# Joining the chain's products with one moving operand in a chunked RWKV-7 recurrence on one core

## The chip, the cores and the metric

The kernel runs on one core of one Trainium2 chip. The metric is the device time of one execution in microseconds (us). TensorE (PE in the profile) multiplies a stationary operand, the weights, by a moving operand; a weight load (PEld) goes ahead of each product. VectorE is DVE, ScalarE is ACT, GpSimd is POOL. Each engine works through its own instructions in the order in which they stand in its program and waits where an operand is not ready.

## The reference, cut to what matters

The reference is a whole layer: projections, a bidirectional RWKV-7 recurrence, an RG-LRU branch, output projections and a mixture of experts. The change lies in the recurrence alone:

```python
def step(s, inp):
    r_t, w_t, k_t, v_t, kk_t, a_t = inp
    s_kk = jnp.einsum('bhvk,bhk->bhv', s, kk_t)
    s = (s * w_t[:, :, None, :] - s_kk[..., None] * (kk_t * a_t)[:, :, None, :]
         + v_t[..., None] * k_t[:, :, None, :])
    return s, jnp.einsum('bhvk,bhk->bhv', s, r_t)
```

There are 16 heads of 64, a forward and a backward pass, 256 context tokens and 1024 latent tokens. Only the latent tokens give an output.

## The kernel before, in words

The recurrence is `phase_b`. It runs in chunks of 64 tokens. A group `n` is 128 tokens (two chunks) of 4 heads in both directions (`e` = 0, 1); there are 40 groups, ten for each of four sets of heads (`pr, g = divmod(n, 10)`), and `g` = 0, 1 are context tokens without an output, `g` > 1 latent tokens with one. For each group and direction `stage_e` makes the scaled keys (`bk`), `stage_i` the scaled queries (`qr`: columns 0 to 63 the key side, 64 to 127 the receptance with which the output is read), the masked products `st1` and `st2`, and the inverse `gf` of the chunk's triangular system, by many small bf16 products (lines 880 and 896). That work doesn't depend on the state.

The state goes through `chain(n)`, which calls `step(n, i)` for the two chunks: 80 steps in all, 64 of them with an output (`out`). One half of the partitions (`h` = 0, 1) of `rv` holds the state and the other half the values v, the other way round for the other `h`; so a product over all 128 partitions of `rv` adds a term of the state and one of v. A step, for each `h` and its four `units` (direction and head):

- line 995: `st1` times `rv` (128 rows by 64 weight columns), the right side of the system; DVE (line 996) and ACT (line 997) copy it to `z`
- line 1011: the receptance half of `qr` times the state in `rv` (64 by 64), the state's part of the output, only in steps with an output
- line 1017: `gf` times `z` (64 by 64), the solve, into the same PSUM columns from which `z` was copied; lines 1018 and 1019 write the result into `rv` in place of the state
- line 1026: one half of `st2` times `rv`, the state's update, to which DVE (line 1028) adds the decayed state `sp` that POOL made (line 1005)
- line 1035: the other half of `st2` times the same `rv`, added to line 1011's result; ACT (line 1039) or DVE (line 1041) takes the output to `y`

PSUM holds one bank (2 KB for each partition) for each `h`, `p2[h]`, of two halves. `start` opens an accumulation: it makes the next products of that bank and those partitions overwrite what stands there, and later ones add.

The order of the work is written out by a small planner: generators yield times, `PERIOD` units to a group, and the instructions get their priorities from these. A group's `stage_i` starts 55 units (`LEAD_I`) ahead of its chain, so three groups ahead, and `qr`, `st1`, `st2` and `pc` have four buffers (`NST`). PE's own order mixes the chain's products with the bf16 products of later groups.

Of the kernel before, what the change touches and what calls it, by code (L numbers as in the profile page):

```python
# [9 lines left out]
F32 = mybir.dt.float32  # L10
# [3 lines left out]
AF = mybir.ActivationFunctionType  # L14
OP = mybir.AluOpType
# [3 lines left out]
P = 128  # L19
# [635 lines left out]
def phase_b(S):  # L655

    nc, tc, A, scr, col, mk = S.nc, S.tc, S.A, S.scr, S.col, S.mk
# [7 lines left out]
    C = 64  # L665
    H = ((slice(0, 64), slice(64, 128)), (slice(64, 128), slice(0, 64)))
    QC = (slice(0, 64), slice(64, 128))
    V, G_, A_ = nc.vector, nc.gpsimd, nc.scalar
# [21 lines left out]
    for e in range(2):  # L690
        m = pk.tile([P, 4, 65], F32, name=f"m65{e}")
# [3 lines left out]
        t = pk.tile([P, 2, 4, 65], F32, name=f"cb{e}")  # L695
# [4 lines left out]
    for i in range(6):  # L700
        t = pk.tile([P, 4, P], BF16, name=f"hmx{i}")
        G_.memset(t, 0.0)
        XH.append(t)
    for i in range(NB):
        X = Prog()
        for nm in ("mid", "lo", "u"):
            t = pk.tile([P, 4, P], BF16, name=f"{nm}x{i}")
# [109 lines left out]
    def stage_i(n, e):  # L817

        pr, g = divmod(n, 10)
        alloc_i(n)  # L820
        G, k = GRP[n], 2 * n + e
        X, xh = XB[k % NB], XH[k % 6]
# [7 lines left out]
        kw = dict(skip_group_check=True)  # L830

        r = new("r", dt=F32, bufs=1)
        hm, mid, lo = new("hm"), new("mid", bufs=3), new("lo", bufs=3)
        for h in range(2):
            sr, tr = H[h]
            pg = front([P, 4, P], "pg")
            for j in range(4):
                cols = slice(0, 128) if g > 1 else slice(0, 64)
                nc.tensor.matmul(pg[:, j, cols], G.bk[sr, e, j, 64 * h:64 * h + 128], G.qr[sr, e, j, cols],  # L839
                                 start=True, stop=True)  # L840
            w = G.st1[:, h, e]
            V.tensor_mul(w, pg[:, :, 0:64], bc(mk("strict", e)))
            A_.activation(hm[sr], w[sr], AF.Copy)  # L843
            G_.tensor_tensor(r[sr], w[sr], hm[sr], op=OP.subtract)  # L844
            A_.activation(w[sr], G.qr[sr, e, :, 0:64], AF.Copy)
            if g > 1:
                V.tensor_mul(G.st2[:, h, e, :, QC[1 - h]], pg[:, :, 64:128], bc(mk("incl", e)))
            yield 1.4
# [16 lines left out]
        for h in range(2):  # L865
            sr, b0 = H[h][0], 64 * h
# [42 lines left out]
        u = u8  # L909
        for it in range(7):  # L910
# [5 lines left out]
            u = pi.tile([P, 4, C], BF16, name="u", tag=f"u{k % NB}")  # L916
# [67 lines left out]
    def step(n, i):  # L984

        pr, g = divmod(n, 10)
        G, T = GRP[n], TILE[pr]
        last, out = g == 9 and i == 1, g > 1
        units = [(e, a, 2 * a + (i if e == 0 else 1 - i)) for e in range(2) for a in range(2)]
        kw = dict(skip_group_check=True)  # L990
        p2 = [psC.tile([P, 2, 2, 2, C], F32, name=f"p2{h}", tag=f"p2{h}") for h in range(2)]
        z = pf.tile([P, 2, 2, C], F32, name="z", tag="z", bufs=1)
        for h in range(2):
            for e, a, j in units:
                nc.tensor.matmul(p2[h][H[h][0], 1, e, a], G.st1[:, h, e, j], G.rv[:, h, e, a, i], start=True, stop=True)
        V.tensor_copy(z[0:64], p2[0][0:64, 1])
        A_.activation(z[64:128], p2[1][64:128, 1], AF.Copy)
        if not last:
            sp = pf.tile([P, 2, 2, C], F32, name="sp", tag="sp", bufs=1)
            for h in range(2):  # L1000
                sr = H[h][0]
                pcs = G.pc[sr].rearrange("p e (a c) -> p e a c", a=2)
                for e in range(2):
                    k = i if e == 0 else 1 - i
                    G_.tensor_tensor(sp[sr, e], G.rv[sr, h, e, :, i],  # L1005
                                     pcs[:, e, :, k:k + 1].to_broadcast([64, 2, C]), op=OP.mult)
        for h in range(2):
            if out:
                sr, tr = H[h]
                for u, (e, a, j) in enumerate(units):  # L1010
                    nc.tensor.matmul(p2[h][tr, 0, e, a], G.qr[sr, e, j, 64:128], G.rv[sr, h, e, a, i],
                                     start=(u == 0), stop=False, **kw)
        yield 3
        for h in range(2):
            sr = H[h][0]
            for e, a, j in units:
                nc.tensor.matmul(p2[h][sr, 1, e, a], G.gf[sr, e, j], z[sr, e, a], start=True, stop=True, **kw)
        V.tensor_copy(G.rv[0:64, 0, :, :, i], p2[0][0:64, 1])
        A_.activation(G.rv[64:128, 1, :, :, i], p2[1][64:128, 1], AF.Copy)
        yield 3  # L1020
        rv, i1 = (G.rv, 1) if i == 0 else (None if last else GRP[n + 1].rv, 0)
        for h in range(2):
            sr = H[h][0]
            if not last:
                for u, (e, a, j) in enumerate(units):
                    nc.tensor.matmul(p2[h][sr, 0, e, a], G.st2[:, h, e, j, QC[h]], G.rv[:, h, e, a, i],
                                     start=(u == 0), stop=(u == 3), **kw)
                V.tensor_tensor(rv[sr, h, :, :, i1], p2[h][sr, 0], sp[sr], op=OP.add)  # L1028
        if out:
            s = 2 * (g - 2) + i  # L1030
            lo_, hi_ = min(s, 15 - s), max(s, 15 - s)
            for h in range(2):
                r = H[h][1]
                for u, (e, a, j) in enumerate(units):
                    nc.tensor.matmul(p2[h][r, 0, e, a], G.st2[:, h, e, j, QC[1 - h]], G.rv[:, h, e, a, i],
                                     start=False, stop=(u == 3), **kw)
                y = T.y[r, :, lo_:hi_ + 1:hi_ - lo_].rearrange("p a e v -> p e a v")
                if s < 8:
                    A_.activation(y, p2[h][r, 0], AF.Copy)
                else:  # L1040
                    V.tensor_tensor(y[:, ::-1], p2[h][r, 0], y[:, ::-1], op=OP.add)
        yield 4

    def finish(n):
# [74 lines left out]
    def alloc_i(n):  # L1119
        G = GRP[n]  # L1120
        if hasattr(G, "st1"):
            return
        pr, g = divmod(n, 10)
        G.pc = pf.tile([P, 2, 4], F32, name=f"pc{n}", tag="pc", bufs=NST)
        G.qr = pf.tile([P, 2, 4, P], F32, name=f"qr{n}", tag="qr", bufs=NST)
        G.st1 = pf.tile([P, 2, 2, 4, C], F32, name=f"st1_{n}", tag="st1", bufs=NST)
        G.st2 = pf.tile([P, 2, 2, 4, P], F32, name=f"st2_{n}", tag="st2", bufs=NST)


# [17 lines left out]
    with ExitStack() as s0:  # L1147
        gp = s0.enter_context(tpool(tc, name="gp", bufs=1))
        load_y(S, "yb", [7], lambda k: gp, S.y)
        for j in range(KT):  # L1150
            n = 59 + j
# [6 lines left out]
            z = product(nc, S.psz.tile([P, 2, 512], F32, name="zb", tag="zl"), S.W.pop(n), S.y)  # L1158
# [4 lines left out]
    pf = pool("pf", 1, side="right")  # L1163
    pi = pool2("pi", 2, side="right")
    psC = pool("psC", 1, space=PSUM)
    psI = pool2("psI", 1, space=PSUM, side="right")
    gnx = pf.tile([64, 32], F32, name="gnx")
    nc.sync.dma_start(gnx, A["gnx"])
    S.early = False
    left = [2 * NG]  # L1170

# [5 lines left out]
    for n in range(NG):  # L1177
        t = n * PERIOD
# [6 lines left out]
    while events:  # L1185
        t, k, gen = heapq.heappop(events)
# [22 lines left out]
NST = 4  # L1209
# [715 lines left out]
```

## Time and profile before

| | |
|---|---|
| median of three runs | 3358.96 us (3342.54 to 3366.52) |
| the profiled execution | 3349.37 us, of which the span is 3347.6 us |
| PE busy | 3021.7 us, 90% of the span |
| DVE busy | 2175.8 us, 65% |
| ACT busy | 1516.2 us, 45% |
| POOL busy | 1237.7 us, 37% |
| mean granted TensorE clock | 0.921 of full speed |

A busy time is an average over stages. The recurrence lies between about 1012 us and 2343 us of the span. The granted clock has two levels, 2.4 GHz (1.0) and 1.2 GHz (0.5); a clock between them in a row is a mean over a stretch that has both. In the trace an fp32 product is two records of PE, two passes over its columns, each with a weight load of its own; a transpose (line 868) and a bf16 product are one. The records' ends are modelled and overlap, so what one record costs is read from the distance of starts, not from its length.

### The profile page before, as it was taken

The numbers are of one execution on the slowest core, as the hardware profiler recorded it, in microseconds if no ns is written. First come the engines' busy times: TensorE is split into PE (matmuls) and PEld (weight loads), VectorE is DVE, ScalarE is ACT, GpSimd is POOL, SyncE is SP. The second block draws the span as 40 slices with busy tenths as digits, with TensorE's granted clock in tenths as the row PEclk, the third lists the DMA queues.
The fourth block names the chain that finished last, engine by engine and source line by source line (L and its number), as shares of the span: only waits on it lengthen the run. The fifth ranks groups of instructions, "written<-read, shape, count | busy, mean of one in ns | idle before, by whom it ended". The sixth has DMA issues, their size and how long they took to land. (4 is left out here: it accounts for less than half of the span.)

```text
span 3347.6 us, 67005 instructions
## 1 busy us (share of the span) xinstructions
PE 3021.7 (90%) x26407; PEld 2288.2 (68%) x26407; DVE 2175.8 (65%) x4155; ACT 1516.2 (45%) x3127; POOL 1237.7 (37%) x1517
## 2 busy tenths in 40 slices
PE   7999998899998999999999999999879599999981
PEld 4877776777777888778878887888767343444430
DVE  6768998977537788888877788877559311111115
ACT  4465556565615666566666665765321000000003
POOL 1022333334416555565455555653113212111114
PEclk9999999999996899899987997989989799999995
DMA  5423336432352111222122112312532788688885
GB/s 213 139 97 120 123 121 202 145 110 77 126 181 83 49 50 48 80 77 60 44 81 71 49 50 76 89 32 80 186 135 100 315 349 341 263 359 320 327 345 218
DMA packets 265464, 496.61 MB, mean 148 GB/s; under 512 B 34690, under 2 KB 188002, under 8 KB 239484
## 3 DMA queue, kind: packets, MB, share of 16 engines
q1 hardware_dynamic: 243804, 443.16, 37.5%
q0 software_dynamic: 21280, 48.28, 3.9%
q8 instruction: 251, 4.11, 0.5%
q14 instruction: 129, 1.06, 0.1%
HBM read 437.37 MB, written 83.83 MB: 156 GB/s over the span
## 5 line engine op out<-in xcount | busy, mean ns | idle before, releaser
L1628 PE MATMUL ph<-r,xT 128*64 128x256 f32 (+1 forms) x2176 | 366.1, 488 | 36.9 <-DVE yo L1652 10.4
L234 PE MATMUL zl<-h_hi,wlo 128*128 128x512 f32 x944 | 328.3, 402 | 17.3 <-DVE wlo L157 17.3
L230 PE MATMUL zl<-h_hi,whi 128*128 128x512 f32 x944 | 327.6, 402 | 3.3 <-ACT acc L408 2.7
L232 PE MATMUL zl<-h_lo,whi 128*128 128x512 f32 x944 | 328.4, 402 | 0.6 <-DVE rstd L287 0.5
L1628 PEld LDWEIGHTS ph<-r,xT 128*64 128x64 f32 x2176 | 165.9, 138 | 231.6 <-issue 186.9
L1653 POOL DMA_INDIRECT scr_yx<-yo,sidx x50 | 50.8, 1016 | 500.8 <-DVE yo L1652 342.8
L839 PE MATMUL pg<-qr,bk 64*128 64x128 f32 (+1 forms) x1280 | 216.8, 315 | 15.8 <-DVE bk L800 6.6
L234 PEld LDWEIGHTS zl<-h_hi,wlo 128*128 128x128 f32 x944 | 180.9, 192 | 55.3 <-DVE wlo L157 19.8
L1617 ACT ACTIVATE xT<-pxt 128x512 f32<-128x512 f32 x37 | 22.1, 597 | 426.1 <-DVE hT L1640 337.6
L230 PEld LDWEIGHTS zl<-h_hi,whi 128*128 128x128 f32 x944 | 180.3, 192 | 43.0 <-issue 3.7
L232 PEld LDWEIGHTS zl<-h_lo,whi 128*128 128x128 f32 x944 | 181.5, 192 | 38.2 <-issue 1.4
L844 POOL TENSOR_TENSOR r<-st,hm 64x256 f32<-64x256 f32 x160 | 115.8, 724 | 240.9 <-ACT hm L843 237.4
L839 PEld LDWEIGHTS pg<-qr,bk 64*128 64x128 f32 x1280 | 182.1, 215 | 30.9 <-issue 6.6
L411 DVE SCALAR_TENSOR_TENSOR acc<-zt,drv,acc 128x960 f32<-128x960 f32 (+3 forms) x142 | 170.7, 1208 | 9.1 <-ACT acc L408 5.4
L1005 POOL TENSOR_TENSOR sp<-rv,pc 64x128 f32<-64x128 f32 x304 | 133.9, 458 | 89.2 <-DVE rv L1028 72.4
L896 PE MATMUL pu<-u,n 128*128 128x64 bf16 x2240 | 157.9, 201 | 3.8 <-DVE n L906 2.2
L157 DVE TENSOR_TENSOR wlo<-wraw,whi 128x1024 fp32r<-128x1024 f32 x67 | 101.1, 1509 | 85.0 <-ACT whi L156 81.2
L896 PEld LDWEIGHTS <-n 128*128 128x128 bf16 x2240 | 125.8, 103 | 36.1 <-issue 15.7
L1640 DVE COPY hT<-pht 128x256 f32<-128x256 f32 x32 | 13.6, 424 | 202.3 <-PE pht L1639 202.2
L918 ACT ACTIVATE u<-pu 128x256 bf16<-128x256 f32 x280 | 104.8, 380 | 84.4 <-PE pu L896 81.1
L920 DVE TENSOR_TENSOR u<-pu,u 128x256 bf16<-128x256 f32 x280 | 114.3, 416 | 25.0 <-PE pu L896 21.5
L783 POOL TENSOR_SCALAR km<-cb,ka 128x128 f32<-128x128 f32 x160 | 96.7, 612 | 75.6 <-ACT cb L777 73.9
(457 smaller groups left out, 8280.5 us busy)
## 6 DMA issues: line engine op xcount, KB each, us to landing
r<-in_e_w_dram SPq DMA_DIRECT2D x192, 1024.0 KB
wraw<-in_w_in_dram SPq DMA_DIRECT2D x59, 512.0 KB
adr<-in_w_ada_dram SPq DMA_DIRECT2D x32, 512.0 KB
zk<-scr_zk SPq DMA_DIRECT2D x80, 128.0 KB
kk<-scr_kk SPq DMA_DIRECT2D x80, 128.0 KB
lp<-scr_lp SPq DMA_DIRECT2D x80, 128.0 KB
v<-scr_zv SPq DMA_DIRECT2D x80, 128.0 KB
wada<-in_w_ada_dram SPq DMA_DIRECT2D x8, 1024.0 KB
```

What stands on the lines that cost most here:

```text
L157: nc.vector.tensor_sub(lo, raw, hi.bitcast(F32))
L230: nc.tensor.matmul(pz, z.hi[:, k], h_hi[:, k, t0:t0 + n], start=(k == 0), stop=False)
L232: nc.tensor.matmul(pz, z.hi[:, k], h_lo[:, k, t0:t0 + n], start=False, stop=False)
L234: nc.tensor.matmul(pz, z.lo[:, k], h_hi[:, k, t0:t0 + n], start=False, stop=(k == KT - 1))
L411: nc.vector.scalar_tensor_tensor(o, i, mures[:n, r, j:j + 1], o, op0=OP.mult, op1=OP.add)
L839: nc.tensor.matmul(pg[:, j, cols], G.bk[sr, e, j, 64 * h:64 * h + 128], G.qr[sr, e, j, cols], start=True, stop=True)
L844: G_.tensor_tensor(r[sr], w[sr], hm[sr], op=OP.subtract)
L896: nc.tensor.matmul(pt[:, j], l[:, j], r_ if len(r_.shape) == 2 else r_[:, j], start=first, stop=True, **kw)
L918: A_.activation(u, pt, AF.Copy)
L920: V.tensor_tensor(u, pt, u8, op=OP.add)
L1005: G_.tensor_tensor(sp[sr, e], G.rv[sr, h, e, :, i], pcs[:, e, :, k:k + 1].to_broadcast([64, 2, C]), op=OP.mult)
L1628: nc.tensor.matmul(ph[HALF[h]].rearrange("p a b c -> p (a b c)")[:, c], x[:, k], w13(e, k)[:, h, c], start=(k == 0), stop=(k == KT - 1))
```

## The change

The diff joins products that have the same moving operand: lines 995 and 1011 both multiply by `rv` before the solve, lines 1026 and 1035 by `rv` after it. `st1` grows from 64 to 128 columns: 64 hold the system's right side as before, the other 64 the receptance half of `qr` on the state's partitions and zeros on the others. One product with 128 weight columns fills both halves of the partitions of the bank. `st2` had both halves already. So that the output's accumulation can go on in one half of the bank, the solve is written to the other half; its `start` makes the update that follows overwrite on the state's partitions.

`st1` is no longer taken from a pool: four tiles `ST1` are set to zero once by POOL, ahead of the stage. ACT's copy out of `qr` (line 845) takes 128 columns in place of 64 where there is an output. `qr` is now read by `stage_i` alone and has one buffer in place of four.

```diff
-            w = G.st1[:, h, e]
+            w = G.st1[:, h, e, :, QC[h]]
             V.tensor_mul(w, pg[:, :, 0:64], bc(mk("strict", e)))
             A_.activation(hm[sr], w[sr], AF.Copy)
             G_.tensor_tensor(r[sr], w[sr], hm[sr], op=OP.subtract)
-            A_.activation(w[sr], G.qr[sr, e, :, 0:64], AF.Copy)
+            if g > 1:
+                w = G.st1[sr, h, e].rearrange("p j (b c) -> p j b c", b=2)
+                A_.activation(w[:, :, ::-1] if h else w, G.qr[sr, e].rearrange("p j (b c) -> p j b c", b=2), AF.Copy)
+            else:
+                A_.activation(w[sr], G.qr[sr, e, :, 0:64], AF.Copy)
...
+        both = slice(0, P)
         for h in range(2):
-            for e, a, j in units:
-                nc.tensor.matmul(p2[h][H[h][0], 1, e, a], G.st1[:, h, e, j], G.rv[:, h, e, a, i], start=True, stop=True)
+            m, c = (both, both) if out else (H[h][0], QC[h])
+            for u, (e, a, j) in enumerate(units):
+                nc.tensor.matmul(p2[h][m, 1, e, a], G.st1[:, h, e, j, c], G.rv[:, h, e, a, i], start=(u == 0), stop=True, **kw)
...
-        for h in range(2):
-            if out:
-                sr, tr = H[h]
-                for u, (e, a, j) in enumerate(units):
-                    nc.tensor.matmul(p2[h][tr, 0, e, a], G.qr[sr, e, j, 64:128], G.rv[sr, h, e, a, i],
-                                     start=(u == 0), stop=False, **kw)
...
-            for e, a, j in units:
-                nc.tensor.matmul(p2[h][sr, 1, e, a], G.gf[sr, e, j], z[sr, e, a], start=True, stop=True, **kw)
-        V.tensor_copy(G.rv[0:64, 0, :, :, i], p2[0][0:64, 1])
-        A_.activation(G.rv[64:128, 1, :, :, i], p2[1][64:128, 1], AF.Copy)
+            for u, (e, a, j) in enumerate(units):
+                nc.tensor.matmul(p2[h][sr, 0, e, a], G.gf[sr, e, j], z[sr, e, a], start=(u == 0), stop=True, **kw)
+        V.tensor_copy(G.rv[0:64, 0, :, :, i], p2[0][0:64, 0])
+        A_.activation(G.rv[64:128, 1, :, :, i], p2[1][64:128, 0], AF.Copy)
...
         for h in range(2):
-            sr = H[h][0]
+            m, c = (both, both) if out else (H[h][0], QC[h])
+            for u, (e, a, j) in enumerate(units):
+                nc.tensor.matmul(p2[h][m, 1, e, a], G.st2[:, h, e, j, c], G.rv[:, h, e, a, i], start=False, stop=True, **kw)
             if not last:
-                for u, (e, a, j) in enumerate(units):
-                    nc.tensor.matmul(p2[h][sr, 0, e, a], G.st2[:, h, e, j, QC[h]], G.rv[:, h, e, a, i],
-                                     start=(u == 0), stop=(u == 3), **kw)
-                V.tensor_tensor(rv[sr, h, :, :, i1], p2[h][sr, 0], sp[sr], op=OP.add)
+                sr = H[h][0]
+                V.tensor_tensor(rv[sr, h, :, :, i1], p2[h][sr, 1], sp[sr], op=OP.add)
...
-                for u, (e, a, j) in enumerate(units):
-                    nc.tensor.matmul(p2[h][r, 0, e, a], G.st2[:, h, e, j, QC[1 - h]], G.rv[:, h, e, a, i],
-                                     start=False, stop=(u == 3), **kw)
...
-        G.qr = pf.tile([P, 2, 4, P], F32, name=f"qr{n}", tag="qr", bufs=NST)
-        G.st1 = pf.tile([P, 2, 2, 4, C], F32, name=f"st1_{n}", tag="st1", bufs=NST)
+        G.qr = pi.tile([P, 2, 4, P], F32, name=f"qr{n}", tag="qr", bufs=1)
+        G.st1 = ST1[n % NST]
...
+    ST1 = [pf.tile([P, 2, 2, 4, P], F32, name=f"st1_{i}") for i in range(NST)]
+    for t in ST1:
+        G_.memset(t, 0.0)
```

The reads of the output (lines 1039 and 1041) take the other half of the bank and are otherwise the same.

The order on PE, at a step's first products and its solve in the middle of the stage. Before (in a row's name, `p_...` is the bank of one `h`, `64x64` the size of the product's result; the bf16 rows of line 896 belong to later groups' inverses):

```order
L896 MATMUL pu<-u,n_19538 128x64
L995 MATMUL p_21175<-rv_20062,st_19_18722 64x64 x4
L1011 MATMUL p_21176<-rv_20062,qr_18721 64x64 x4
L1017 MATMUL p_21176<-z,gf_19880 64x64 x4
L896 LDWEIGHTS n_19538
```

After, the first products of a step (lines 918, 872, 884 and 900 are lines 914, 868, 880 and 896 of before, lines 1001 and 1025 the joined products):

```order
L884 MATMUL ph<-x_18131,n_17913 128x8
L1001 MATMUL p_18756<-rv_17773,st_0_7303 128x64 x4
L872 MATMUL pt<-ident,bk_18540 128x64 x4
L1001 MATMUL p_18757<-rv_17773,st_0_7303 128x64 x4
L918 LDWEIGHTS idb
L918 MATMUL pu<-u_17696,idb 128x256
```

The solve of the same step, some 35 rows further on:

```order
L884 LDWEIGHTS n_17913
L884 MATMUL ph<-x_18182,n_17913 128x8
L1017 MATMUL p_18756<-z,gf_17600 64x64 x4
L1017 MATMUL p_18757<-z,gf_17600 64x64 x4
L900 LDWEIGHTS n_17305
L900 MATMUL pu<-u,n_17305 128x64
```

Line 1011's product no longer stands between the first products and the solve; the first products' results are 128 by 64 and lie among products of the same 128 by 128 weights, and the solve alone keeps 64 by 64.

The order on POOL at the stage's start (`km`, `bk` and `pc` are the keys and decays of the first groups, `rv` the state that is set to zero). Before:

```order
L798 TENSOR_TENSOR bk_6658<-km,ip 128x4x64
L814 COPY pc_7303<-pp 128x4
L1106 MEMSET rv_8008 64x2x64 x3
L862 TENSOR_TENSOR bk_7367<-bk_6658,pc_7303 128x4x128
L1106 MEMSET rv_8008 64x2x64
L1005 TENSOR_TENSOR sp<-rv_8008,pc_7303 64x128 x2
```

After (line 1103 is line 1106 of before):

```order
L798 TENSOR_TENSOR bk_6658<-km,ip 128x4x64
L1169 MEMSET st_0_7303 128x2048
L1169 MEMSET st_1_7304 128x2048
L1169 MEMSET st_2_7305 128x2048
L1169 MEMSET st_3_7306 128x2048
L814 COPY pc_7311<-pp 128x4
L1103 MEMSET rv_8014 64x2x64 x4
```

The four new settings to zero stand between the first group's keys and its `pc`, `rv` and `sp`.

## Rows read from the trace of the kernel before

**Rows 1.** Windows over the recurrence: us, then busy (instructions) by engine, clock, DMA.
```profile
1041.00:2343.00 1302.00, 1229.91 (x17430) 1068.50 (x17429) 1062.42 (x2721) 823.96 (x2217) 716.79 (x1102) 0.89 0.22 62
1000.00:1200.00 200.00, 182.85 (x2156) 158.43 (x2154) 146.14 (x369) 115.64 (x311) 113.72 (x180) 0.78 0.21 62
1200.00:1400.00 200.00, 187.07 (x2837) 162.75 (x2836) 170.94 (x437) 130.76 (x354) 115.53 (x175) 0.95 0.23 66
1600.00:1800.00 200.00, 187.43 (x2523) 161.28 (x2523) 164.12 (x410) 125.78 (x330) 117.15 (x177) 0.86 0.25 72
```

**Rows 2.** Waits, 1041 to 2343 us: waiter <- releaser, us in total, times, longest.
```profile
PE pu L914 <- DVE u L920: 9.4, 12, 2.0
...
DVE st L842 <- PE pg L839: 53.7, 57, 3.0
```

**Rows 3.** Groups by line and form, 1000 to 2345 us: count, busy us, mean ns, idle before.
```profile
L995 PE MATMUL p<-rv,st 128*64 128x64 f32 x1280 | 118.5, 242 | 2.2 <-DVE y L1041 1.8
L1026 PE MATMUL p<-rv,st 128*64 128x64 f32 x1216 | 106.3, 246 | 1.8 <-DVE rv L1018 1.2 <-ACT rv L1019 0.2
L1017 PE MATMUL p<-z,gf 64*64 64x64 f32 x1280 | 105.5, 237 | 0.0
L1011 PE MATMUL p<-rv,qr 64*64 64x64 f32 x1024 | 87.6, 232 | 0.5 <-DVE z L996 0.5
L1035 PE MATMUL p<-rv,st 128*64 128x64 f32 x1008 | 86.6, 242 | 1.8 <-DVE rv L1028 1.4
L845 ACT ACTIVATE st<-qr 64x256 f32<-64x256 f32 x160 | 65.9, 412 | 24.2 <-POOL r L844 21.6
L777 ACT ACTIVATE cb<-pl 128x512 f32<-128x512 f32 x79 | 47.0, 595 | 46.9 <-PE pl L775 41.1 <-DVE ip L799 4.9 <-DVE hmx L855 0.3
L811 DVE TENSOR_TENSOR qr<-pp,kk 128x256 f32<-128x256 f32 x80 | 43.2, 541 | 8.4 <-ACT pp L795 4.1 <-PE p L1011 3.4
L1106 POOL MEMSET rv<- 64x128 f32 x16 | 2.8, 198 | 63.6 <-PE zb L1242 59.6 <-PE p L1035 3.7
```

**Rows 4.** PE in order of time: start, us, line, tiles, weights, moving, records.
```profile
1503.32 0.56 PE L995 MATMUL p<-rv,st 128*64 128x64 f32 x6
1503.82 0.40 PE L896 MATMUL pv<-t,hmx 128*128 128x128 bf16 x4
1504.14 0.33 PE L995 MATMUL p<-rv,st 128*64 128x64 f32 x2
...
1504.51 0.57 PE L1017 MATMUL p<-z,gf 64*64 64x64 f32 x7
```

**Rows 5.** The same view in a later stage, the router's products.
```profile
2516.63 0.73 PE L1490 MATMUL plg<-rw,xT 128*128 128x36 f32 x5
2517.18 0.28 PE L1480 MATMUL px<-vv,po 128*128 128x64 bf16 x4
2517.30 0.39 PE L1490 MATMUL plg<-rw,xT 128*128 128x36 f32 x2
2517.53 0.48 PE L1506 MATMUL z<-wo_hi,m_hi 128*128 128x512 f32 x1
```

**Rows 6.** One record's length by line: least, median, most ns.
```profile
L1017 PE MATMUL p<-z,gf x1280: 218/218/366, 1089.8 to 2343.7; 64*64 64x64 f32 x183
L1490 PE MATMUL plg<-rw,xT x128: 194/279/407, 2501.2 to 2612.3; 128*128 128x36 f32 x128
```

**Rows 7.** POOL's setting to zero of 1024 columns, whole span.
```profile
L383 POOL MEMSET ada<- 128x1024 f32 x4 | 3.8, 957 | 0.3 <-issue 0.3
```

**Rows 8.** Windows: a stretch at the full clock and the one behind it at half.
```profile
1549.00:1658.30 109.30, 105.30 (x1636) 91.72 (x1635) 93.42 (x240) 71.55 (x195) 59.37 (x98) 1.00 0.18 53
1658.30:1685.60 27.30, 27.30 (x264) 23.36 (x264) 15.93 (x44) 12.68 (x32) 11.47 (x14) 0.50 0.19 54
```

**Rows 9.** Windows: the last 5 us before two falls of the clock.
```profile
1393.90:1398.90 5.00, 3.46 (x60) 2.88 (x57) 4.91 (x13) 4.53 (x13) 1.47 (x2) 1.00 0.11 31
1653.30:1658.30 5.00, 2.73 (x50) 2.28 (x48) 4.73 (x13) 3.48 (x11) 1.27 (x5) 1.00 0.03 8
```

More of the change, by code (lines that the diff above doesn't have):

```diff
@@ L1033, in step @@
                 r = H[h][1]
-                for u, (e, a, j) in enumerate(units):
-                    nc.tensor.matmul(p2[h][r, 0, e, a], G.st2[:, h, e, j, QC[1 - h]], G.rv[:, h, e, a, i],
-                                     start=False, stop=(u == 3), **kw)
                 y = T.y[r, :, lo_:hi_ + 1:hi_ - lo_].rearrange("p a e v -> p e a v")
                 if s < 8:
-                    A_.activation(y, p2[h][r, 0], AF.Copy)
+                    A_.activation(y, p2[h][r, 1], AF.Copy)
                 else:
-                    V.tensor_tensor(y[:, ::-1], p2[h][r, 0], y[:, ::-1], op=OP.add)
+                    V.tensor_tensor(y[:, ::-1], p2[h][r, 1], y[:, ::-1], op=OP.add)
         yield 4
```

## The prediction

> **What bounds the kernel now.** The change lies in the recurrence, so I read the windows over that stage first, then who waits for whom, then PE in order of time, last the clock. In 1302 us PE is busy 1229.91 us (94.5%), DVE 1062.42 (81.6%), ACT 63%, POOL 55% [rows 1]. PE's longest wait comes to 9.4 us in all, while DVE waits 53.7 us for one line of PE [rows 2]. So PE's throughput sets most of the stage, and 80 steps in 1302 us (16.3 us each) leave the chain's own latency room. The stage's granted clock is 0.89 [rows 1]; with levels of 1.0 and 0.5 that is a share of 2 x (1 - 0.89) = 0.22 of the time at half. At the full clock PE starts 1636 records in 109.3 us (15.0 per us), at half 264 in 27.3 us (9.7) [rows 8]: a microsecond at half does 0.65 of one at full, and a stage with a share h at half runs at a pace of 1 - 0.35h, now 0.923.
>
> **The change, part by part.** The sum is made against the profiled execution, 3349.37 us; the median of the runs shown is 9.6 us above it.
>
> *Records.* Seven records of line 1017 (64 weight columns, 64 moving) take 0.57 us [rows 4], of which the last one's length is 0.218 [rows 6]: (0.57 - 0.218) / 6 = 0.059 us from start to start. A joined product has 128 weight columns and 64 moving ones, which the recurrence doesn't show. The nearest row is the router's: 128 weight columns and only 36 moving ones, five records in (0.73 - 0.279) / 4 = 0.113 us each [rows 5, 6]. Fewer moving columns cost more there, so the weights set the distance. The ends are 0.059 (moving columns alone count) and 0.113; I take 0.113, since the row has the same weights. Line 1011 has 1024 records; line 1035 has 1024 too (64 steps of 16; a few are missing in the trace) [rows 3]. Line 1026 has 1216 = 76 x 16, none in the last step of each set of heads, where the joined product stays for the output alone. So 1024 + 1024 - 64 = 1984 records go: -1984 x 0.059 = -117 us. The 64 steps with an output keep 32 joined records each, which grow: 2048 x 0.054 = +111 us. Net -6 us: by weight columns, joining saves next to nothing.
>
> The Trainium skill, page "TensorE: Matmul & The Clock Gate", section "LDWEIGHTS (loading the stationary operand)", says the same against this change: a load's time goes by its columns, P / 1.2 ns, which makes 107 ns here (an estimate). [...]
>
> *Switches of shape.* Six records of line 995 stand from 1503.32 to 1503.82 [rows 4]: 0.50 us where six times 0.059 are 0.35. The 0.15 more is the slow first record and the change back to a product over 128 weight columns. Four records of line 896 then take 0.32 us up to the next line 995, with 128 moving columns each; four with 64 take 0.12 ahead of line 1490, which has 128 by 128 weights [rows 5], so twice that is 0.24, and 0.08 is the way in. One visit to the narrow shapes costs 0.15 + 0.08 = 0.23 us. Between line 1490 and bf16 products nothing of the kind is to be seen: five records in 0.55 us, 0.11 each, and the way back at 0.03 per record [rows 5]. The joined products have that shape. Counted in the two orders, the chain's products are entered over a switch of shape 602 times before and 284 times after: 318 x 0.23 = -73 us. The other narrow products (lines 839 and 868) lose neighbours of similar shape: 53 switches more, at about 0.09, +5 us. Net -68 us. So the gain lies in fewer changes of shape, not in fewer columns.
>
> Sum on PE: -6 - 68 = -74 us at the full clock, -74 / 0.923 = -80 at the present mix. The ends are -80 (PE bounds everywhere) and 0 (each us becomes a wait for DVE). Ahead of two falls of the clock DVE was busy 4.91 and 4.73 of 5 us and PE 3.46 and 2.73 [rows 9]: there are stretches that DVE sets. PE's 94.5% against 81.6% says most are PE's; I take two thirds, -53 us, a stage of 1249 us.
>
> *ACT.* 128 of the 160 copies of line 845 double to 512 elements: 412 ns now, 595 ns for line 777 with 512 [rows 3]. The ends are 0 and +412; I take +183: 23 us of ACT, 63% to 65%. Hidden, since their reader runs three groups later; with that cover gone, 23 us at most.
>
> *POOL at the start.* Four settings of 2048 columns, by the 957 ns for 1024 [rows 7] 1.9 us each, 7.7 in all. POOL sat idle 59.6 us before line 1106 for the projection's last products [rows 3], so tiles whose space is free earlier cost nothing, those that wait for the same products push `pc`, `rv` and `sp` back. Ends 0 and 7.7; I take 3.
>
> *`qr` in one buffer.* The 3.4 us that DVE waited at line 811 for line 1011 [rows 3] go. The new wait, for line 839 and ACT's copy of the group before, comes 18 planner units after these were issued: 0. If it did bite, the DVE work queued behind line 811 would stand, and PE's products that need it; by the old wait a few us. *The solve in the other half* is the same instructions: 0. `z`'s first half comes 8 x 0.054 = 0.43 us later, but line 1011 no longer stands ahead of the solve: 0.
>
> *The clock.* PE's stream gets thinner: a joined record streams 64 columns in 0.113 us, where 64 took 0.059. 17430 - 1984 = 15446 records in 1249 us are 12.4 per us, against 13.4. In the stage's stretches 14.2 per us went with a clock of 0.95, 12.6 with 0.86, 10.8 with 0.78 [rows 1], and before falls PE had 12 and 10 per us, at busy shares of 69% and 55%, against 96% in the stretch at full [rows 8, 9]. Which of the two draws the other the rows don't settle. The ends are 0.89 (no change) and 0.78 (the thinnest stretch). I take 0.84, a little under the nearest row: h = 0.32, pace 0.888, 1249 x 0.923 / 0.888 = 1298 us.
>
> The Trainium skill's same page, Part 1, says that the clock is low by default and that recent activity of PE releases it. The falls behind a half-idle PE agree with it [rows 9].
>
> Total: 1298 - 1302 + 3 = -1 us: about 3348 us in the profiled execution's terms, 3355 with part of the median's distance. **Forecast: no change that can be measured**; the switches' gain is given back by the clock.
>
> **Rivals.**
> 1. *The clock stays at 0.89.* -53 + 3 = -50: 3299 us. For it: without switches the bf16 products stand closer, and in rows 1 a low clock itself thins the stream. Against: rows 9. Faster by 1% begins at a stage of 1265 us, pace 0.911, a clock of about 0.87.
> 2. *The clock falls as far as in the stage's thinnest stretch, 0.78.* h = 0.44, pace 0.846, 1249 x 0.923 / 0.846 = 1363: +64 with POOL's 3, 3413 us, slower. It decides below a clock of about 0.81 (pace 0.866 for a stage of 1332). For it: joined records load weights half of the time; DVE-set stretches get more frequent as PE gets faster. Against: fewer switches close gaps in PE.
> 3. *By moving columns alone.* Joined records stay 0.059 us apart: -117 in place of -6, so -185 with the switches, -200 at the mix of clocks, two thirds -134, with POOL's 3 about 3218 us. The router's records [rows 5, 6] all but exclude it. [...]
> 4. *It doesn't pay at all:* all of PE's gain becomes waits for DVE, at a clock of 0.86: 1302 x 0.923 / 0.902 = 1332, +33, 3382 us.
>
> **How the numbers follow.** One per cent, 33 us, is about what a measurement of this kernel can tell from no change. The likeliest case, a clock between 0.81 and 0.87, has 0.47 and a range of its own of 3325 to 3385; rival 1 has 0.23 and rival 3 0.02, together faster 0.25; rival 2 has 0.20 and rival 4 0.08, slower 0.28. The range 3298 to 3408 takes in most of rivals 1, 2 and 4 and leaves out rival 3 and the ends beyond.
>
> **What would show it.** Joined records 0.11 us apart in PE's order of time, with no slow change beside bf16 products; 1984 records fewer; a granted clock of about 0.84 over the recurrence; ACT's line 845 near 595 ns; line 811 without waits for PE. A step of 0.06 us would make records and rival 3 right; a clock of 0.89 with the stage near 1250 us rival 1; more DVE waits of PE at an unchanged clock rival 4. The prediction fails if PE's gain lands in full, or if the clock moves otherwise than its rows suggest.

## The result, and the profile after

The changed kernel takes 3542.47 us (median of four runs, 3523.70 to 3571.09) against 3353.28 us, a ratio of **1.056** with an interval of 1.050 to 1.061. The forecast was 3355 us with a range of 3298 to 3408. The direction of rival 2 came true, and more of it than its price.

Each ratio in this document leaves out runs over 1.5% above the fastest of the same kernel, and is against runs of the kernel before taken beside it (medians 3353.28 us here, 3362.55 for experiments 1 to 4, 3366.06 for 5 to 8, 3378.99 for 9 and 10, 3366.61 for 11 and 12), so it isn't the quotient of the medians given. The traces show one execution each: the changed kernel's is its longest (3571.09 us, with a granted clock of 0.847 over the whole, where the other three have 0.856 to 0.859), so its clock is a low reading, and the two traces are 222 us apart where the medians are 189.

The windows over the recurrence, its columns as in [rows 1]: the whole stage, then single stretches, of which the last six are a stretch at the full clock, its last 5 us, a stretch at half soon behind it, one of the two longest at half, and the last 5 us before another fall with the stretch at half that follows.

```profile
1045.00:2552.00 1507.00, 1420.13 (x15439) 1274.67 (x15438) 1067.78 (x2727) 849.83 (x2214) 702.01 (x1099) 0.72 0.19 54
1200.00:1400.00 200.00, 191.31 (x1939) 175.53 (x1938) 127.98 (x334) 103.84 (x277) 81.88 (x138) 0.66 0.14 40
1800.00:2000.00 200.00, 183.27 (x2158) 163.24 (x2157) 152.97 (x386) 121.89 (x314) 110.93 (x167) 0.79 0.26 74
1860.00:1921.40 61.40, 52.79 (x794) 45.87 (x793) 55.71 (x136) 45.92 (x119) 47.07 (x69) 1.00 0.35 100
1916.40:1921.40 5.00, 2.73 (x49) 2.34 (x48) 4.91 (x11) 2.04 (x6) 4.78 (x9) 1.00 0.37 107
1935.10:1965.80 30.70, 30.70 (x241) 28.03 (x240) 14.69 (x43) 14.72 (x39) 10.24 (x18) 0.50 0.06 18
2296.90:2375.40 78.50, 78.02 (x627) 69.94 (x626) 38.09 (x107) 34.36 (x87) 25.25 (x47) 0.50 0.10 27
2138.30:2143.30 5.00, 5.00 (x64) 4.65 (x62) 3.44 (x12) 2.59 (x7) 1.35 (x2) 1.00 0.01 2
2143.30:2160.40 17.10, 17.05 (x135) 15.23 (x135) 10.73 (x29) 7.85 (x21) 3.58 (x7) 0.50 0.00 1
```

The longest stretch at half in the kernel before:

```profile
1805.00:1846.00 41.00, 40.46 (x404) 35.47 (x403) 24.22 (x71) 17.85 (x50) 13.53 (x22) 0.50 0.08 24
```

Against [rows 1] the stage is 205 us longer, 1991 PE records fewer, DVE's busy time the same, and the clock 0.72 instead of 0.89. The fall at 1921 us came like those of [rows 9], behind 5 us in which DVE was busy for 4.91 and PE for 2.73; most falls in both traces are of this kind, but the one at 2143 us came behind 5 us in which PE was busy for all 5.00. At half, PE is busy for 30.70 of 30.70 and 78.02 of 78.50 us, and still isn't given the full clock. That is not new: in the kernel before PE was busy for 27.30 of 27.30 us at half [rows 8], and for 40.46 of 41.00 in the longest such stretch. What is new is how much of it there is: 30 stretches at half begin in the stage, 26.4 us each, where 22 of 13.2 us did; the longest grew from 41 to 78.5 us. The page's row of the clock shows the same in its middle, where before it reads `6899899987997989989`:

```profile
PEclk9999999999976666678778777856999799999996
```

PE in order of time (columns of [rows 4]), first at the full clock, then at half:

```profile
2484.65 2.00 PE L1025 MATMUL p<-rv,st 128*128 128x64 f32 x16
...
2492.38 1.08 PE L1025 MATMUL p<-rv,st 128*128 128x64 f32 x8
2493.30 0.28 PE L900 MATMUL ps<-u,ux 128*128 128x64 bf16 x4
2493.42 1.08 PE L1025 MATMUL p<-rv,st 128*128 128x64 f32 x8
```
```profile
2311.57 0.40 PE L900 MATMUL pr<-t,lox 128*128 128x64 bf16 x4
2311.78 1.95 PE L1025 MATMUL p<-rv,st 128*128 128x64 f32 x8
2313.53 0.40 PE L884 MATMUL ph<-x,n 128*128 128x8 bf16 x8
```

Sixteen joined records take 2.00 us, the last one's length is 0.314 (the median of line 1025): (2.00 - 0.314) / 15 = 0.112 us, the predicted 0.113. Eight of them, with the way into bf16, take 0.92 us, and the four bf16 records behind them 0.12: no switch of shape is left there. At half, eight take 1.75 us, 0.22 each. So a joined product moves 64 columns in 0.112 us at the full clock and in 0.22 at half, where [rows 4] had 64 in 0.059.

Lines (as in [rows 3]) and DVE's longest waits (as in [rows 2]):

```profile
L1001 PE MATMUL p<-rv,st 128*128 128x64 f32 x1024 | 200.1, 358 | 2.3 <-ACT y L1036 1.2 <-DVE y L1038 1.0
L847 ACT ACTIVATE st<-qr 64x512 f32<-64x512 f32 x128 | 79.9, 624 | 16.3 <-POOL r L844 14.7
L811 DVE TENSOR_TENSOR qr<-pp,kk 128x256 f32<-128x256 f32 x80 | 47.6, 599 | 2.1 <-ACT pp L795 1.7
L1169 POOL MEMSET st<- 128x2048 f32 x2 | 3.6, 1811 | 47.6 <-PE zb L1243 47.6
```
```profile
DVE st L842 <- PE pg L839: 94.8, 79, 5.6
DVE rv L1028 <- PE p L1025: 80.7, 69, 3.8
```

ACT's copy takes 624 ns (forecast 595), line 811 no longer waits for PE, a setting to zero takes 1.8 us (1.9), and the stage starts 4 us later (3). DVE now waits 94.8 us at line 842, 53.7 before: it is PE that is late, not DVE.

**One measure for all runs.** With h, the share of the stage at half clock summed from the granted clock, length x (1 - 0.35 h) is what the stage would take at the full clock by the prediction's pace model. Before: h = 0.225, 1302 x 0.921 = 1200 us. After: h = 0.561, 1507 x 0.804 = 1211 us. By this model all but 14 of the 205 us are the clock's: (1200 / 0.804) - 1302 = 190. The experiments below are held against this measure, called L. Taken the same way over the whole span, with h as 2 x (1 - granted clock), every execution whose clock is on record, of every kernel below that gives the full output, comes to 3160 to 3198 us, and the executions of one kernel differ by up to 15 us. So a difference in L of some ten us between two traces decides nothing.

### The profile page after: what moved, and what is told of

Read it like the earlier page. It is cut to its first block, busy times and chain, and to the rows that moved or that the text cites. A ratio compares the mean times of both kernels' runs of the same rounds, so it can differ in the third digit from the quotient of the medians.

```text
span 3569.1 us, 63103 instructions
## 1 busy us (share of the span) xinstructions
PE 3215.6 (90%) x24423; PEld 2498.9 (70%) x24423; DVE 2181.5 (61%) x4155; ACT 1544.3 (43%) x3127; POOL 1229.8 (34%) x1521
## 5 line engine op out<-in xcount | busy, mean ns | idle before, releaser
L839 PE MATMUL pg<-qr,bk 64*128 64x128 f32 (+1 forms) x1280 | 259.1, 357 | 19.1 <-DVE bk L800 10.6
L839 PEld LDWEIGHTS pg<-qr,bk 64*128 64x128 f32 x1280 | 217.8, 252 | 39.3 <-POOL bk L798 8.8
L1001 PE MATMUL p<-rv,st 128*128 128x64 f32 (+1 forms) x1280 | 227.0, 338 | 2.7 <-ACT y L1036 1.2
L1025 PE MATMUL p<-rv,st 128*128 128x64 f32 (+1 forms) x1280 | 223.6, 341 | 2.1 <-DVE rv L1018 1.8
L1001 PEld LDWEIGHTS p<-rv,st 128*128 128x128 f32 (+1 forms) x1280 | 203.4, 245 | 12.9 <-issue 2.7
L1025 PEld LDWEIGHTS p<-rv,st 128*128 128x128 f32 (+1 forms) x1280 | 204.5, 249 | 8.5 <-DVE rv L1018 2.1
L900 PEld LDWEIGHTS <-n 128*128 128x128 bf16 x2240 | 146.9, 113 | 51.3 <-issue 26.1
L900 PE MATMUL pu<-u,n 128*128 128x64 bf16 x2240 | 176.0, 214 | 7.3 <-DVE n L910 5.8
```

What stands on the lines that cost most here:

```text
L900: nc.tensor.matmul(pt[:, j], l[:, j], r_ if len(r_.shape) == 2 else r_[:, j], start=first, stop=True, **kw)
L1001: nc.tensor.matmul(p2[h][m, 1, e, a], G.st1[:, h, e, j, c], G.rv[:, h, e, a, i], start=(u == 0), stop=True, **kw)
L1025: nc.tensor.matmul(p2[h][m, 1, e, a], G.st2[:, h, e, j, c], G.rv[:, h, e, a, i], start=False, stop=True, **kw)
```

## The experiments

**1. The columns doubled.** Both joins stay, but each joined product streams its 64 columns twice, into both halves of the bank; the second copy is overwritten or not read. Weights, records and order are those of the changed kernel.

```diff
-                nc.tensor.matmul(p2[h][m, 1, e, a], G.st1[:, h, e, j, c], G.rv[:, h, e, a, i], start=(u == 0), stop=True, **kw)
+                x = G.rv[:, h, e, a, i][:, None, :].to_broadcast([P, w.stop - w.start, C])
+                nc.tensor.matmul(p2[h][m, w, e, a], G.st1[:, h, e, j, c], x, start=(u == 0), stop=True, **kw)
```

and the same at line 1025; `w` is both halves where there is an output.

> The changed kernel, but the joined products stream their 64 moving columns twice, into both halves of the bank (the second copy is never read): 128 moving columns for each record. Line 839 of the kernel before has fp32 records of 128 weight columns with 128 and with 64 moving ones, 0.112 us apart either way, so the records should cost PE no more. Clock theory (the joined records leave PE's moving side half idle and the clock is granted less; 0.72 over the recurrence): the granted clock of the recurrence comes back to 0.87 to 0.93, the recurrence takes about 1250 us and the whole 3290 to 3320 us, below the kernel before. Weights theory (the wide loads themselves fill PE): nothing changes, 3520 to 3570 us. Structure theory (one qr buffer, ACT's wider copy, the solve in the other half, the other order): nothing changes either, 3520 to 3570 us.

Measured: 3359.13 us, ratio 0.9967 (0.9935 to 0.9999). The windows over its recurrence:

```profile
1046.50:2348.50 1302.00, 1194.56 (x15449) 1064.82 (x15448) 1070.81 (x2727) 844.15 (x2214) 705.00 (x1099) 0.89 0.21 62
```

PE does more, nothing reads the addition, and 183 us come back: the clock is 0.89 again, h = 0.213. That decides for the clock as the cause of the loss. It also shows a second miss, since the whole was expected at 3290 to 3320 us. At before's clock the stage is 1302 us, as before: PE's busy time fell from 1229.91 [rows 1] to 1194.56, by 35 us, and PE's idle time rose from 72 to 107, by the same 35.

**2 to 4. The joins one by one.** Both undone (every other edit kept), then only the products ahead of the solve joined, then only those behind it. The edit of experiment 2, for line 1001 (line 1025 likewise, its other half back where line 1035 stood):

```diff
-            m, c = (both, both) if out else (H[h][0], QC[h])
...
-                nc.tensor.matmul(p2[h][m, 1, e, a], G.st1[:, h, e, j, c], G.rv[:, h, e, a, i], start=(u == 0), stop=True, **kw)
+                nc.tensor.matmul(p2[h][H[h][0], 1, e, a], G.st1[:, h, e, j, QC[h]], G.rv[:, h, e, a, i], start=(u == 0), stop=True, **kw)
...
+                    nc.tensor.matmul(p2[h][tr, 1, e, a], G.st1[sr, h, e, j, QC[1 - h]], G.rv[sr, h, e, a, i],
+                                     start=(u == 0), stop=True, **kw)
```

> The changed kernel with both joins undone and all else kept: st1 tiles set to zero once, ACT's wide copy, one qr buffer, the solve in the other half of the bank; the output's products run on their own with 64 weight columns, in the places where they ran before. Clock theory: the clock of the recurrence comes back to about 0.89 and the time to 3345 to 3375 us, that of the kernel before. Weights theory: the same. Structure theory: the time stays at 3500 us or more.

> Only the products ahead of the solve are joined (st1 with the receptance); the two after it run apart as before. Clock theory: the 1024 records that go had 64 rows, so PE's stream loses the lesser part; the recurrence's clock is between, about 0.83, and the time 3390 to 3440 us. Weights theory: half of the loss, about 3450 us at an unchanged clock of 0.89. Structure theory: 3500 us or more.

> Only the products after the solve are joined (both halves of st2); the two ahead of it run apart as before. Clock theory: the 960 records that go had 128 rows, the greater part of what PE's stream loses; the recurrence's clock is about 0.78 and the time 3440 to 3500 us, above the kernel with only the first products joined. Weights theory: half of the loss, about 3450 us at an unchanged clock. Structure theory: 3500 us or more.

Measured: 3410.11 us, 1.0108 (1.0060 to 1.0155); 3401.52, 1.0115 (1.0019 to 1.0210); 3496.70, 1.0368 (1.0278 to 1.0459). The three windows, in this order:

```profile
1048.20:2406.60 1358.40, 1287.48 (x17442) 1115.97 (x17441) 1069.72 (x2729) 847.70 (x2214) 708.57 (x1099) 0.85 0.21 59
```
```profile
1049.90:2355.50 1305.60, 1224.98 (x16405) 1081.14 (x16403) 1066.35 (x2730) 849.57 (x2217) 718.08 (x1099) 0.88 0.22 63
```
```profile
1048.00:2489.40 1441.40, 1355.48 (x16481) 1194.23 (x16480) 1066.86 (x2729) 846.28 (x2215) 709.58 (x1099) 0.77 0.20 57
```

The structure theory's 3500 us is out by experiment 2, and experiments 3 and 4 came within the times that the clock theory gave. The join behind the solve costs most: alone it makes 3.7%, while the join ahead alone costs nothing that can be told from experiment 2 (1.0115 and 1.0108) and, added to the other, takes the ratio from 1.037 to 1.056. The one takes out line 1035's products, over all 128 partitions, the other line 1011's, of 64; that this is the reason was expected and fits, but no run separates it from the joins' different places. L is 1212, 1192 and 1212 us: again the clock (h = 0.309, 0.250, 0.455) makes the difference. That the kernel without any join is 1.1% slower, with the products of before, was not foreseen. (Experiment 3's profiled execution, 3364.81 us, is the fastest of its four; its window is read for L alone.)

**5 to 7. Columns elsewhere.** Line 880's 2240 bf16 products move 8 columns each; in all three kernels they stream them seven times, and line 882 reads the first copy alone. This is put on the kernel before, on experiment 1 and on the changed kernel.

```diff
-                ph = psum([P, 8, 8], "ph")
+                ph = psum([P, 8, 7, 8], "ph")
...
-                    nc.tensor.matmul(ph[:, q], G.n8[q // 4][:, q % 4], i8b if it == 0 else x8[:, q], start=True, stop=True)
+                    nc.tensor.matmul(ph[:, q], G.n8[q // 4][:, q % 4],
+                                     (i8b if it == 0 else x8[:, q])[:, None, :].to_broadcast([P, 7, 8]), start=True, stop=True)
...
-                V.tensor_tensor(x8, ph, mk("i8")[:, None, :].to_broadcast([P, 8, 8]), op=OP.add)
+                V.tensor_tensor(x8, ph[:, :, 0], mk("i8")[:, None, :].to_broadcast([P, 8, 8]), op=OP.add)
```

> The kernel before with one edit: line 880's products stream their 8 moving columns seven times over, into a result tile seven times as wide, of which line 882 reads the first copy alone. No weight load, no product and no result changes; the 2240 products stream 56 columns in place of 8. So far every run fits one rule: length of the recurrence x (1 - 0.35 h), with h the share at half clock, is 1191 to 1212 us whatever was joined (before 1302 x 0.921 = 1199; after 1507 x 0.804 = 1212; joined with columns doubled 1205; split 1211). Theory 1 (the clock follows how many columns PE streams, and the clock sets the time): the clock over the recurrence rises from 0.89 to 0.93 or more, h to 0.14 or less, stage 1201 / 0.951 = 1263 us or less, whole about 3310 us, ratio 0.985. Theory 2 (the thinner stream and the low clock of the changed kernel both come from waits, columns as such count for nothing): clock 0.89, time the same or up to 2240 x 0.02 = 45 us longer, ratio 1.000 to 1.013.

> The changed kernel with both joins and doubled moving columns in them (as in the first experiment) and line 884's 8 columns streamed seven times. Theory 1 with the PE gain lost to other engines (the recurrence at full clock takes about 1200 us whatever PE saves): clock of the stage 0.93 or more, stage about 1260, whole about 3315 us, ratio to before 0.985, and no better than the kernel before with the wide products. Theory 1 with the predicted PE gain alive (it was only hidden by the clock): about 50 us less, 3265 us, ratio 0.972. Theory 2 (columns count for nothing): the same as the first experiment, ratio 0.997 to 1.01.

> The changed kernel as it is (joined products stream their 64 columns once) with line 884's 8 columns streamed seven times. Theory 1: a part of the loss comes back with work added that nothing reads; clock of the stage from 0.72 to about 0.80 (h 0.40), stage 1212 / 0.86 = 1409 us, whole about 3440 us, ratio 1.026. Theory 2: clock 0.72, 3540 to 3585 us, ratio 1.055 to 1.07.

Measured: 3308.89 us, 0.9839 (0.9805 to 0.9873); 3337.48, 0.9909 (0.9880 to 0.9938); 3482.23, 1.0397 (1.0306 to 1.0488). The windows:

```profile
1045.10:2299.80 1254.70, 1186.04 (x17434) 1027.75 (x17432) 1063.52 (x2723) 823.17 (x2218) 715.68 (x1102) 0.94 0.23 65
```
```profile
1051.70:2331.90 1280.20, 1175.89 (x15451) 1047.68 (x15451) 1067.88 (x2728) 843.91 (x2212) 707.87 (x1099) 0.92 0.22 62
```
```profile
1047.20:2441.10 1393.90, 1287.29 (x15446) 1153.93 (x15446) 1062.98 (x2727) 843.09 (x2213) 714.67 (x1099) 0.82 0.20 59
```

Work added that nothing reads makes both kernels faster, the clock going from 0.89 to 0.94 and from 0.72 to 0.82. L stays: 1204, 1207, 1217 us. Joining gives nothing even where the clock is 0.92 to 0.94; the second theory, that columns as such count for nothing, is out. The first theory's size for experiment 7, about 3440 us, was too low by 42 us, and its window is of the fastest of its four executions (3452.67 us), so 0.82 is a high reading of its clock.

**8. Less work on PE.** The kernel of experiment 5 without line 1011's products, so without the state's part of the output:

```diff
...
-                    nc.tensor.matmul(p2[h][tr, 0, e, a], G.qr[sr, e, j, 64:128], G.rv[sr, h, e, a, i],
-                                     start=(u == 0), stop=False, **kw)
...
-                                     start=False, stop=(u == 3), **kw)
+                                     start=(u == 0), stop=(u == 3), **kw)
```

> The kernel before without line 1011's 1024 records and with line 880's 8 columns streamed seven times, to be held against the kernel before with the wide products alone. It leaves out the state's part of the output (line 1035 opens the accumulation in its place). If PE's throughput bounds the recurrence at full clock: 1024 x 0.059 = 60 us and most of 128 visits' 0.23 us, 29 us, leave PE, so length x (1 - 0.35 h) falls from about 1200 to about 1120. If another engine's pace or the chain's own length bounds it there: it stays within 15 us of 1200 and PE's saving turns into idle time. The clock in either case is no higher than in the kernel before with the wide products (fewer columns), so the time is 3310 to 3340 us in the second case and 3230 to 3260 in the first.

Measured: 3287.00 us, 0.9762 (0.9719 to 0.9804).

```profile
1043.40:2302.10 1258.70, 1164.82 (x16426) 1007.88 (x16425) 1070.19 (x2723) 819.70 (x2215) 723.42 (x1102) 0.91 0.22 64
```

Both ends missed: L is 1176 us, 28 under experiment 5, where 1120 or 1200 was expected. And the stage is 4 us longer than experiment 5's with 1008 records fewer seen, since the clock fell from 0.94 to 0.91. The whole is shorter all the same, for 21 us behind the stage (from its end to the span's end 985 us, in experiment 5 1007). There the experts do less: how many blocks of tokens each takes depends on the router's counts (`tc.If(n > 64)` and on), and with a part of the output left out 2048 records of their first products stand where experiment 5 has 2176. So the ratio of 0.9762 doesn't price the recurrence; L does. Experiment 5, then 8:

```profile
L1629 PE MATMUL ph<-r,xT 128*64 128x256 f32 (+1 forms) x2176 | 365.3, 487 | 37.4 <-PEq L1687 14.0
L1623 PE MATMUL ph<-r,xT 128*64 128x256 f32 (+1 forms) x2048 | 351.5, 494 | 35.7 <-PEq L1681 12.2
```

**9 to 11. Is it DVE?** Line 813 goes to POOL and the expanded copy of `lo` to ACT, on experiment 5, on experiment 6, and on one with only the products ahead of the solve joined, columns doubled.

```diff
-                V.tensor_mul(G.qr[:, e, :, 64:128], inc, c4(r))
+                G_.tensor_tensor(G.qr[:, e, :, 64:128], inc, c4(r), op=OP.mult)
...
-                V.tensor_copy(o[QC[h], :, QC[h]], x[QC[h]])
+                cp(o[QC[h], :, QC[h]], x[QC[h]], act)
...
-        expand(X.lo, lo)
+        expand(X.lo, lo, True)
```

> The kernel before with line 880's 8 columns streamed seven times, and two pieces of DVE's work given to others: line 813 (62 seen at 537 ns, 33 us) to POOL and the expanded copy of lo (156 at 320 ns, 50 us) to ACT. DVE loses 83 of its 1063 us in the recurrence; PE's work is that of the kernel before with the wide products. Theory A (DVE and PE share the bound at full clock, so what PE saves becomes waits for DVE): length x (1 - 0.35 h) falls from 1204 to about 1165, half of the 83, and PE's idle time from 69 us to about 35; whole about 3265 us, ratio 0.971. Theory C (DVE has no part in it): 1200, ratio 0.982 to 0.986.

> The changed kernel with both joins, doubled moving columns in them, line 884's columns streamed seven times, and the same two pieces of DVE's work given to POOL and ACT. To be held against the run above. Theory A: with DVE out of the way the 35 us of PE's busy time that joining saved, lost as idle time so far (PE idle 104 us against 69), come back: length x (1 - 0.35 h) from 1207 to about 1135, 25 us or more under the run above. Theory B (joining frees no PE time that the stage can use, since a joined product also makes the chain longer for those who wait for it): within 12 us of the run above, PE's idle time still some 30 us longer. Theory C: about 1205. The whole by A about 3250 us, by B about 3285 us (its clock was lower than the other's), by C 3335 us.

> Only the products ahead of the solve joined, with their moving columns doubled; the products behind it apart as before; line 884's 8 columns streamed seven times; the two pieces of DVE's work on POOL and ACT as in the two runs before. Of the three kernels that differ from it in one thing, the one without a join had 1206 us of length x (1 - 0.35 h) and 3303.5 us, the one with both joins 1195 and 3310.7. If a join frees PE time that the stage can use (theory A): about 1185 us, ratio 0.970 to 0.975. If not (theory B): 1195 to 1210 us at a clock of about 0.95, ratio 0.980 to 0.985, no better than without a join.

Measured: 3303.52 us, 0.9810 (0.9743 to 0.9878); 3310.72, 0.9832 (0.9765 to 0.9899); 3289.55, 0.9776 (0.9714 to 0.9838).

```profile
1041.70:2290.50 1248.80, 1171.93 (x17444) 1016.60 (x17442) 1014.70 (x2507) 875.85 (x2371) 757.30 (x1165) 0.95 0.22 64
```
```profile
1047.30:2284.90 1237.60, 1139.62 (x15452) 1015.39 (x15451) 1000.01 (x2506) 892.33 (x2369) 747.17 (x1165) 0.95 0.22 64
```
```profile
1045.70:2278.60 1232.90, 1155.28 (x16409) 1014.58 (x16409) 1008.64 (x2505) 905.60 (x2370) 760.02 (x1165) 0.96 0.23 65
```

DVE lost 49 us of the 83: others of its instructions ran longer, line 857's from 535 to 588 ns, with POOL and ACT busier (757 us against 716, 876 against 823); why was not tested. Without a join L is 1206, as it was (1204), where half of 49 us would have brought it to about 1180: theory A falls there, DVE alone was not the bound. With both joins L goes from 1207 to 1195. At one clock, 0.95, the joined kernel's stage is 11 us shorter and PE's idle time still 98 us against 77: theory B, at the edge of its 12 us, which is also no more than executions of one kernel differ by; by the medians (3310.72 and 3303.52 us) the joined kernel is no faster. Experiment 11 gives L = 1198. Its whole time is the lowest of a kernel with the full output, but its interval overlaps those of experiments 5 and 9, so a gain of the one join over none isn't shown. Experiment 5 alone, a few lines, has most of it.

**12. ACT's copy.** Line 845 done twice in the kernel before:

```diff
-            A_.activation(w[sr], G.qr[sr, e, :, 0:64], AF.Copy)
+            for _ in range(2 if g > 1 else 1):
+                A_.activation(w[sr], G.qr[sr, e, :, 0:64], AF.Copy)
```

> The kernel before with ACT's copy of line 845 done twice where there is an output: 128 x 412 ns = 53 us more ACT work at the place where the changed kernel has 128 x 212 = 27 us more. If this copy is what made the kernel with both joins undone 1.1% slower: at least that much here, ratio 1.011 to 1.025, with a clock of the recurrence of 0.85 or less. If ACT's extra work is hidden, as the prediction said: ratio 0.997 to 1.004, clock 0.89.

Measured: 3384.61 us, ratio 1.0039 (1.0000 to 1.0077). Twice the extra ACT work costs at most 0.8%, so the copy is hidden for the most part and hardly the 1.1% of experiment 2. (Its profiled execution, 16 us above the median and at a stage clock of 0.86, doesn't decide on the clock.)

## Why the prediction was wrong

**The step that failed is the clock's size.** "I take 0.84, a little under the nearest row" was 0.72, below even the lower end of 0.78: h of 0.56 in place of 0.32. The mechanism was the prediction's own (joined records stream 64 columns in 0.113 us and the stream gets thinner), and rival 2 named its place. The ends were read from stretches of the kernel before, whose low-clock stretches still held the old products. That PE can be busy throughout at half clock and be kept there stood in [rows 8] already, with 27.30 of 27.30 us; the prediction took its pace from that row and for the clock read only the falls behind a partly idle PE [rows 9]. What no row before could show is how much longer such stretches get once the joined records fill them, which take 0.22 us at half for the same 64 columns. That the fewer columns for each record are the cause is shown by experiment 1; how they keep the clock down is not. Put into the prediction's sum, h = 0.56 alone makes 1249 x 0.923 / 0.804 = 1434 us of the stage, 136 more than the 1298 it gave.

The Trainium skill's page "TensorE: Matmul & The Clock Gate", Part 1, has the clock follow how busy PE has recently been. The falls of [rows 9] agree; the fall behind 5.00 us of busy PE and the 78 us at half with PE busy for 78.02 don't, if busy is read as the profile's busy time. There the measurement decides: doubled columns at the same records and the same weights brought 0.72 back to 0.89.

**The second failed step is "two thirds realised".** The -53 us came to nothing: L is 1192 to 1217 us in every kernel with the full output, 1200 before. That is the other 73 us (1507 - 1434). To see where the terms went, I took the distances between starts of PE's records at the full clock, cut at 215 ns, and scaled them to L; what is beyond the cut is waiting:

| us | before | experiment 1 | forecast |
|---|---|---|---|
| between two of the chain's records | 312 | 323 | -6 |
| into and out of the chain's products | 173 | 120 | -73 |
| beside line 839 | 172 | 181 | +5 |
| all other records | 466 | 476 | 0 |
| beyond 215 ns | 77 | 106 | a third of the gain |
| sum (L) | 1200 | 1206 | |

The switches were worth 53, not 73: by the medians of these distances the way into a narrow product takes 0.123 us and the way back to bf16 0.154, against 0.058 and 0.029 without a switch, so a visit costs 0.19 us and not 0.23, and the trace of experiment 1 has 299 visits where the one before has 576, 277 fewer and not 318. The records cost 11 more instead of 6 less, the two other rows grew by 19, and the waits took 29, six more than was left. That is rival 4's place at an unchanged clock, though not for its reason: taking work from DVE freed nothing (experiment 9), and of line 1011's records and switches, priced at 89 us, only 28 came through (experiment 8). So neither PE's nor DVE's throughput alone sets the stage at the full clock. What does was not settled; "PE's throughput sets most of the stage", read from 94.5% busy [rows 1], was too strong.

**Right:** the records' 0.112 us against rival 3's 0.059, the end of the switches beside bf16 products, ACT's 624 ns, POOL's start, the waits of line 811, and the pace model: L lies within 1.5% of 1200 us at clocks from 0.72 to 0.96. The Trainium skill's page "TensorEngine Tiling (Array Packing)", section "Key Properties", says that a change of tiling mode drains TensorE; the 0.123 us into a narrow product and 0.154 out of it agree, and so do the 173 us into and out of the chain's products, 120 with the joins. **Not foreseen:** the clock of 0.85 with both joins undone. One buffer for `qr` shows no wait there, and the copy's price alone is too small; what in the rest (the order of the work, the solve's other half) lowers the clock stays open.

## What to carry to other kernels

Where PE's clock moves within a stage, take the length apart into what it would be at the full clock and the share at half before pricing an edit; here the second moved by 190 us and the first by 11. An edit that made products stream fewer columns for their weight load slowed a stage here in which PE was 94% busy and stayed so, and the test for it is cheap: stream the same columns twice and look at the granted clock. A high busy share of one engine doesn't say that work taken from it comes out of the time; take some out and look at its idle time.

## What was not expected of the hardware

Streaming columns that nothing reads made the kernel before 1.6% faster (3308.89 us, 0.9839), with the stage's clock at 0.94 instead of 0.89. PE stayed at half clock for 78.5 us while its records covered 78.02 of them, and fell to half at 2143 us out of 5 us that they covered whole. A joined record took about as long with 128 moving columns as with 64; in PE's order of time of experiment 1, at the full clock:

```profile
1847.40 1.14 PE L1027 MATMUL p<-rv,st 128*128 128x128 f32 x8
1848.37 0.28 PE L900 MATMUL pt<-i64b,ux 128*128 128x64 bf16 x4
```

Eight records take 0.97 us up to the next product, 0.121 each, where eight of 64 columns took 0.92 (2492.38 to 2493.30 above): twice the columns for 5% more time.
